# The first eight weight units of a hybrid mixer as two seven-product block multiplications, and convolution taps of two channel tiles by turns

## The chip, the core and the metric

The kernel runs on one core of a Trainium2 chip. The metric is the device time of one execution in microseconds (us), as the median of several runs. The engines of the core are named as in the profile: PE (TensorE, matmuls), PEld (its weight loads), DVE (VectorE), ACT (ScalarE), POOL (GpSimd) and SP (SyncE, which here only issues DMA transfers).

## The reference, cut to what matters

The program is a two-layer trunk for 512 frames and 16 meta tokens (T = 528) of width 1024, in float32. Each layer adds half a SwiGLU feed-forward, a mixer, and half a second feed-forward, each behind an RMSNorm.

```python
def hybrid_mixer(u, w_in, ...):
    proj = u @ w_in
    q, k, v, a, b, g_sb, g_conv = jnp.split(proj, IN_SPLITS, axis=-1)
    y_sb = stick_breaking_attention(q, k, v) @ w_attn_out
    y_conv = conformer_conv(a, b, conv_w, conv_b, conv_ln_g, conv_ln_b) @ w_conv_out
    m = jax.nn.sigmoid(g_sb) * y_sb + jax.nn.sigmoid(g_conv) * y_conv
    return m @ w_out
...
def conformer_conv(a, b, conv_w, conv_b, ln_g, ln_b):
    u = a * jax.nn.sigmoid(b)
    y = causal depthwise convolution of u, 31 taps, 512 channels, + conv_b
    return jax.nn.silu(layernorm(y, ln_g, ln_b))
```

The change concerns a and b, the value and gate halves of the GLU (512 channels each, four tiles of 128), and the 31 taps of the convolution behind it.

## The kernel before, in words

**Numbers in two halves.** Activations lie transposed: 128 channels by 528 tokens a tile, eight tiles u[0..7] for the width of 1024. Each operand of a matmul is split into a rounded part hi and a rest lo (`split`, L77: ScalarE copies hi, VectorE subtracts), and a product is three matmuls: hi·hi, hi·lo, lo·hi. Tokens go in two halves of 264 columns.

**Units.** Weights come as units, tiles of 128 x 8 x 128 (512 KB), listed in `units` (L130 to L155) in the order of use. `unit` (L243) hands out the next one and prepares up to three ahead (`LOOK`). `prep_unit` (L213) makes hi and lo in four buffers each (tags wh, wl). Mixer units get hi by a ScalarE copy (L224), a negated hi by another (L225), and an accumulating DMA from POOL's queue that adds the weight to it (L226), which is lo. Other units use `split`. `fetch` (L179) loads raw units through SP's queue into three buffers (tag wr), in the order of `fetches`.

**Seven products for eight.** From the third or fifth channel tile on, the feed-forwards multiply gate and up weights of two channel tiles as a 2 x 2 block system: two halves of the width by two channel tiles, against two halves of the width by two halves of the tokens. `quad` (L566) does this with seven products, w11, s1, s2, w21, s3, w22, s4 (`QUAD`), where the s are sums of weight blocks; each product is 2 x 4 x 3 = 24 matmuls (L580). `fetch_sums` (L196) loads s1 and s3 by a plain DMA (L208) and an accumulating one on POOL's queue (L210); s2 and s4 are further VectorE additions (L236). The sums of activations that they need are made by `sums` (L365): two ScalarE copies, four VectorE operations and two splits for each of four pairs of tiles. For the feed-forward behind a mixer, and for the one behind a whole layer, three of the four are made in the tail ahead of it (`prepare`, L326) and the last in `head` (L517), whose two plain tiles (L502) come ahead of the blocks.

**The mixer** (L678). At its start the residual h is stored to DRAM (L687). The GLU loop (L760 to L774) takes, for each of four channel tiles, unit b (both token halves, 48 matmuls, L706) and unit a (one half after the other, 48 matmuls, L720). After the first b the RMSNorm's scale is computed (L409, four matmuls with a matrix of ones, then `rsqrt`, L391). VectorE multiplies by that scale (L726), ScalarE takes the sigmoid, POOL multiplies (L773) into the padded tile uc. Then attention runs with the products q, k, v and the gates in its gaps, in an order of TensorE written out by hand (L987), and then the post stage (L998): last gate unit, attention output (ao, 4 units), the convolution's LayerNorm (L1029 to L1056), two gate units, convolution output, output projection.

**The taps.** `conv_some` (L736) issues VectorE's taps (L748, each multiplies a shifted uc by a column and adds y to it) at the lowest priority behind an evacuation: 31 taps of one channel tile after the other, about two for each evacuation of 264 columns (`CONV_STEP` = 4). What is left when the first attention-output unit is done (`AO_FIRST` = 1) comes before the LayerNorm (L1028). `constants` (L288) loads tables that attention needs; the first feed-forward calls it (L546).

Outside hand-written orders the compiler places the instructions of each engine in one queue, by priority and by its own estimate of when their inputs are ready.

Of the kernel before, what the change touches and what calls it, by code (L numbers as in the profile page):

```python
# [13 lines left out]
P = 128  # L14
# [19 lines left out]
CONV_STEP = 4  # L34
# [4 lines left out]
AO_FIRST = 1  # L39
# [21 lines left out]
def kernel(ctx, tc, hT, par, const, wg1, wu1, wd1, win, wao, wco, wout, wg2, wu2, wd2, out):  # L61
# [15 lines left out]
    def split(x, hi, lo):  # L77

        act.copy(hi, x)  # L79
        dve.tensor_tensor(out=lo, in0=x, in1=f(hi), op=ALU.subtract)  # L80

# [14 lines left out]
    def fn(out, in_, func, **kw):  # L96
# [8 lines left out]
        table["acts"].append(i)  # L105

# [3 lines left out]
    RAW_OF = {"w11": (0, 0), "w22": (1, 1), "w12": (0, 1), "w21": (1, 0)}  # L110
# [19 lines left out]
    units = []  # L130
    for l in range(DEPTH):
        for fi, (wg, wu, wd) in enumerate(((wg1, wu1, wd1), (wg2, wu2, wd2))):
            if fi == 1:
                for i in range(4):
                    units += [(("b", l, i), win[l, 16 + i], 8), (("a", l, i), win[l, 12 + i], 8)]
# [23 lines left out]
    ready, raws, spared = {}, {}, set()  # L159
    quads = {"pool": None, "of": None}  # L160

    def pieces(n, block=None):

        key, src, nk = units[n]
        if nk in QUAD:
            wg, wu, m = src
            k, c = RAW_OF[block or nk]
            return [(4 * e, 4 * e + 4, w[m + c, :, 4 * k:4 * k + 4]) for e, w in enumerate((wg, wu))]
# [3 lines left out]
    fetches = []  # L172
    for n, (key, src, nk) in enumerate(units):
        if nk == "w11":
            fetches += [n, n + 5, n + 3]
        elif nk not in QUAD:
            fetches.append(n)

    def fetch(spare=None):  # L179

        while state["fetch"] < len(fetches) and (spare or state["out"] < RAW):
            n = fetches[state["fetch"]]
            state["fetch"] += 1
            if spare:
                raw = spare
                spared.add(units[n][0])
            else:
                state["out"] += 1
                raw = wpool.tile([P, 8, P], F32, tag="wr", bufs=RAW, name="wr")
            for a, b, src in pieces(n):  # L190
                nc.sync.dma_start(raw[:, a:b], src)
            raws[units[n][0]] = raw
            if spare:
                return

    def fetch_sums():  # L196

        n = state["sums"]
        while n < len(units) and units[n][2] != "w11":
            n += 1  # L200
        if n == len(units) or units[n][0][1:3] != quads["of"]:
            return
        state["sums"] = n + 1
        _, *at = units[n][0]
        for name, first in (("s1", "w11"), ("s3", "w22")):
            t = quads["pool"].tile([P, 8, P], F32, tag=name, bufs=2, name=name)
            for a, b, src in pieces(n, first):
                nc.sync.dma_start(t[:, a:b], src)  # L208
            for a, b, src in pieces(n, "w12"):
                pool.dma_start(t[:, a:b], src, accum_op=ALU.add)  # L210
            raws[(name, *at)] = t

    def prep_unit():  # L213
# [7 lines left out]
        if nk not in QUAD:  # L221
            raw = raws.pop(key)
            if key[0] in MIXER:
# [925 lines left out]
```

## Time and profile before

| | us |
|---|---|
| runs of the kernel before | 2151.03, 2152.31, 2152.36 |
| their median | 2152.31 |
| span of the profiled execution | 2150.5 |
| mixer's GLU stage in layer 0, first to last matmul | 368.3 to 415.5 |
| the same in layer 1 | 1445.2 to 1492.4 |

The profiled execution's own time is its span, 2150.5 us, and the little before its first and behind its last instruction. The first table of the profile lists the busy time of each engine and the number of its instructions. A list of waits says which engine waited for whom. The chain of waits follows the work that ended last back through what released it. A table by stretches gives, for a stretch of the span, each engine's busy time (x instructions), the granted TensorE clock, the mean busy share of the 16 DMA engines and GB/s. A timeline row is start, length, engine, line, operation, out<-in, and in brackets the idle time before it with what ended that. For groups of DMA transfers the time to landing runs from issue to the last byte.

### The profile page before, as it was taken

The page shows a single profiled execution, that of the slowest core. Times are in us where ns is not written, and L with a number is a line of the kernel's source. Part 1 is how long each engine was busy: PE and PEld are TensorE (multiplying, and loading weights), DVE is VectorE, ACT ScalarE, POOL GpSimd, SP SyncE. Part 2 cuts the span into 40 slices and gives each one's busy share as a digit, 9 for nine tenths or more (in the row PEclk, how much of TensorE's full clock was granted, in tenths as well). Part 3 has the DMA queues.
Part 4 walks back from the last instruction along what each step waited for, and adds up shares of the span by engine and source line. Part 5 has one row for each costly group of instructions (what it writes and reads, how often), then busy time and mean ns, then how long its engine had stood idle before and what let it go on. Part 6 is the DMA issues. An engine that isn't in the chain of part 4 may idle for free.

```text
span 2150.5 us, 39932 instructions
## 1 busy us (share of the span) xinstructions
PE 2135.9 (99%) x16226; PEld 2052.8 (95%) x16226; DVE 1521.5 (71%) x2091; ACT 1137.9 (53%) x1587; POOL 488.7 (23%) x449
## 2 busy tenths in 40 slices
PE   9999999999999999999999999999999999999998
PEld 9999999999999999999999999999888889999897
DVE  7867685677766777677877676856677767767685
ACT  6434355467776545343554443554778775444354
POOL 1322321211111131313113223212112111322320
PEclk9999999999999999999999999999999999999999
DMA  8465536865578747464365655368656886665542
GB/s 236 133 165 141 142 104 198 181 138 119 134 169 180 175 129 189 129 161 122 99 169 145 168 140 146 103 193 184 142 127 133 187 188 167 159 175 143 144 111 77
DMA packets 140168, 324.90 MB, mean 151 GB/s; under 512 B 15568, under 2 KB 19664, under 8 KB 139984
## 3 DMA queue, kind: packets, MB, share of 16 engines
q1 hardware_dynamic: 101856, 226.36, 33.3%
q0 software_dynamic: 37440, 95.44, 26.1%
q8 instruction: 127, 2.08, 0.4%
q10 hardware_dynamic: 688, 0.55, 0.1%
q14 instruction: 57, 0.47, 0.1%
HBM read 315.86 MB, written 6.42 MB: 150 GB/s over the span
## 4 chain that ended last, share of the span: by engine, by line
PE 99%; ACT 0%; DVE 0%; DMA 0%; issue 0%; DVEq 0%; ACTq 0%
PE pb L580 16%; PE ps L580 16%; PE ps L720 15%; PE ps L260 12%; PE ps L706 10%; PE pe L260 6%; PE pb L260 6%; PE pe L580 5%; PE z L706 2%; PE ps L502 2%; PE pe L502 1%; PE pb L502 1%; PE z L877 1%; PE po L921 1%; PE z L900 1%; PE ps L554 1%
## 5 line engine op out<-in xcount | busy, mean ns | idle before, releaser
L79 ACT CAST wh<-wr 128x1024 fp32r<-128x1024 f32 (+4 forms) x275 | 242.2, 887 | 372.4 <-PE ps L260 94.5
L80 DVE TENSOR_TENSOR wl<-wr,wh 128x1024 fp32r<-128x1024 f32 (+4 forms) x275 | 300.6, 1096 | 57.4 <-ACT wh L79 53.5
L79 ACT CAST wh<-s 128x1024 fp32r<-128x1024 f32 x158 | 165.8, 1049 | 274.9 <-DVE s L236 83.1
L80 DVE TENSOR_TENSOR wl<-s,wh 128x1024 fp32r<-128x1024 f32 x158 | 216.1, 1368 | 59.4 <-ACT wh L79 58.7
L720 PE MATMUL ps<-uh,wh 128*128 128x264 f32 (+1 forms) x792 | 243.8, 308 | 0.0
L720 PE MATMUL ps<-uh,wl 128*128 128x264 f32 (+1 forms) x792 | 240.0, 303 | 0.0
L720 PE MATMUL ps<-ul,wh 128*128 128x264 f32 (+1 forms) x792 | 239.9, 303 | 0.0
L640 POOL TENSOR_TENSOR h<-h,dt 128x528 f32<-128x528 f32 (+1 forms) x96 | 179.9, 1879 | 258.1 <-DVE dt L638 255.2
L210 POOL DMA_DIRECT2D s<-wg x78 | 72.8, 938 | 596.9 <-DMA s<-wg 337.9
L748 DVE SCALAR_TENSOR_TENSOR y<-uc,prm,y 128x528 f32<-128x528 f32 (+1 forms) x240 | 197.7, 824 | 4.1
L224 ACT CAST wh<-wr 128x1024 fp32r<-128x1024 f32 x104 | 109.1, 1049 | 141.2 <-issue 46.9
L580 PE MATMUL ps<-ul,wh 128*128 128x264 f32 (+1 forms) x624 | 177.4, 284 | 0.0
L580 PE MATMUL pb<-sl,wh 128*128 128x264 f32 (+1 forms) x624 | 176.9, 283 | 0.0
L580 PE MATMUL ps<-uh,wl 128*128 128x264 f32 (+1 forms) x624 | 176.9, 283 | 0.0
L580 PE MATMUL pb<-sh,wl 128*128 128x264 f32 (+1 forms) x624 | 176.8, 283 | 0.0
L580 PE MATMUL pb<-sh,wh 128*128 128x264 f32 (+1 forms) x624 | 176.5, 283 | 0.0
L580 PE MATMUL ps<-uh,wh 128*128 128x264 f32 (+1 forms) x624 | 176.2, 282 | 0.0
L720 PEld LDWEIGHTS ps<-uh,wl 128*128 128x128 f32 x792 | 149.1, 188 | 5.9
L720 PEld LDWEIGHTS ps<-uh,wh 128*128 128x128 f32 x792 | 148.9, 188 | 5.4
L720 PEld LDWEIGHTS ps<-ul,wh 128*128 128x128 f32 x792 | 149.0, 188 | 5.1
L260 PE MATMUL ps<-ah,wh 128*128 128x264 f32 (+1 forms) x616 | 142.0, 300 | 0.0
L260 PE MATMUL ps<-ah,wl 128*128 128x264 f32 (+1 forms) x616 | 141.8, 300 | 0.0
(319 smaller groups left out, 6460.8 us busy)
## 6 DMA issues: line engine op xcount, KB each, us to landing
wr<-wd SPq DMA_DIRECT2D x96, 384.0 KB, 3.6
wr<-win SPq DMA_DIRECT2D x72, 512.0 KB, 4.4
wl<-win POOLq DMA_DIRECT2D x72, 512.0 KB, 7.8
wr<-wg SPq DMA_DIRECT2D x117, 256.0 KB, 3.0
wr<-wu SPq DMA_DIRECT2D x117, 256.0 KB, 3.4
s<-wg SPq DMA_DIRECT2D x78, 256.0 KB, 5.2
s<-wu SPq DMA_DIRECT2D x78, 256.0 KB, 5.7
s<-wg POOLq DMA_DIRECT2D x78, 256.0 KB, 5.2
```

Source lines behind the costliest of these rows:

```text
L79: act.copy(hi, x)
L80: dve.tensor_tensor(out=lo, in0=x, in1=f(hi), op=ALU.subtract)
L210: pool.dma_start(t[:, a:b], src, accum_op=ALU.add)
L224: act.copy(hi[:, :nk], raw[:, :nk])
L260: pe.matmul(ps[:, c, :n], wt[:, k0 + k, :], xt[:, s:s + n], start=(k == 0 and pi == 0), stop=(k == end and pi == 2))
L502: pe.matmul(ps[:, e, :TH], wt[:, k, :], xt[:, s], start=(k == ORDER[0] and pi == 0), stop=(k == ORDER[-1] and pi == 2))
L554: pe.matmul(ps[:, e, :TH], wt[:, k, :], xt[:, s], start=(k == 0 and pi == 0), stop=(k == KD - 1 and pi == 2))
L580: pe.matmul(ps[:, e, :TH], wt[:, 4 * e + kk, :], xt, start=start and kk == 0 and pi == 0, stop=kk == 3 and pi == 2, skip_group_check=True)
L640: pool.tensor_tensor(out=tri(h[j], mode), in0=tri(h[j], mode), in1=tri(t, mode), op=ALU.add)
L706: pe.matmul(ps, wt[:, k0 + k, :], xt[:, s], start=(n == 0 and pi == 0), stop=(n == nk - 1 and pi == 2))
L720: pe.matmul(ps, wt[:, k, :], xt[:, s], start=(n == 0 and pi == 0), stop=(n == KD - 1 and pi == 2))
L748: t = dve.scalar_tensor_tensor(out=y, in0=uc[i][:, c0 + k:k + T], scalar=col(w0 + k), in1=y, op0=ALU.mult, op1=ALU.add)
```

## The change

It does four things.

1. The eight GLU units of a layer become two block systems of the kind above: pair 0 has channel tiles 0 and 1, pair 1 has 2 and 3, with gate (b) in the place of gate and value (a) in that of up. The seven products of both pairs are interleaved in one hand-written order (`OPENING`), 14 products of 24 matmuls. The unit names o11 and o21 stand for w11 and w21 where they are loaded as plain units. The norm's matmuls come between the two first products and the third.
2. The sums that the blocks need are made in the tail of the feed-forward ahead (three pairs) and behind the norm (the last).
3. Taps go by turns between the two channel tiles of a pair, and start when a pair is done; `CONV_STEP` is 5 and `AO_FIRST` 2.
4. `constants` is called in the mixer of layer 0 into a temporary tile, not in the first feed-forward; identity is loaded apart.

```diff
-CONV_STEP = 4
+URGENT = 200
+CONV_STEP = 5
...
-AO_FIRST = 1
+AO_FIRST = 2
...
+    OPENING = (("o11", 0), ("o11", 1), ("o21", 0), ("s1", 0), ("s2", 0), ("o21", 1), ("w22", 0), ("s3", 0), ("s1", 1),
+               ("s4", 0), ("s2", 1), ("s3", 1), ("w22", 1), ("s4", 1))
...
-                for i in range(4):
-                    units += [(("b", l, i), win[l, 16 + i], 8), (("a", l, i), win[l, 12 + i], 8)]
+                units += open_pair((2, l), [(win[l, 16:20], win[l, 12:16], m) for m in (0, 2)])
...
     for n, (key, src, nk) in enumerate(units):
+        at = key[1:]
         if nk == "w11":
-            fetches += [n, n + 5, n + 3]
+            later_sums.append((n, ("s1", "s3")))
+            fetches += [(n, (name, *at), name) for name in ("w11", "w22", "w21")]
+        elif nk == "s1" and at in opened:
+            first = units[n - 1][2] in OPEN
+            later_sums.append((n, ("s3",) if first else ("s1", "s3")))
+            fetches += [(n, key, nk)] if first else []
+        elif at in opened and nk in ("s2", "s4"):
+            fetches.append((n, ("w22" if nk == "s2" else "w21", *at), "w22" if nk == "s2" else "w21"))
         elif nk not in QUAD:
-            fetches.append(n)
+            fetches.append((n, key, nk))
+
+    def load(raw, n, *blocks):
+
+        for queue, block, kw in zip((nc.sync, pool), blocks, ({}, {"accum_op": ALU.add})):
+            for a, b, src in pieces(n, block):
+                queue.dma_start(raw[:, a:b], src, **kw)
...
-            if key[0] in MIXER:
+            raw, nk0, nk = raws[key], nk, 8 if nk in OPEN else nk
+            if key[0] in MIXER or nk0 == "o11" or nk0 == "o21" and units[n - 1][2] == "o11":
                 act.copy(hi[:, :nk], raw[:, :nk])
                 act.activation(lo[:, :nk], raw[:, :nk], AF.Copy, scale=-1.0)
-                pool.dma_start(lo[:, :nk], src[:, :nk].bitcast(F32R), accum_op=ALU.add)
+                for a, b, src in pieces(n):
+                    pool.dma_start(lo[:, a:b], src.bitcast(F32R), accum_op=ALU.add)
...
-            split(raws[("s1" if nk in ("s2", "s4") else nk, *at)], hi, lo)
+            i = split(raws[("s1" if nk in ("s2", "s4") else nk, *at)], hi, lo)
+            if nk == "s3" and at in opened:
+                tc.add_manual_dep(i.ins, state["rsqrt"].ins.name, NOSYNC, reason="behind the norm")
...
+    def pair(ptile, sp, st, mode, of, ats, between, take, done):
...
+        As = [ptile() for _ in range(2)]
+        ws = [unit("o11", *of, at) for at in ats]
+        for ks in (range(KH - 1), (KH - 1,)):
+            for A, w in zip(As, ws):
+                products(A, w, x(0, 0), True, ks)
+        Bs = [ptile("pb")]
+        begin(Bs[0], v(As[0]))
+        between(ptile("pe"), copies[0])
+        Bs.append(kept(As[1]))
+        q, E, c22 = {}, {}, {}
+
+        def step(name, n):
+            w = unit(name, *of, ats[n])
+            if name == "o21":
+                products(As[n], w, x(0, 1))
+                take(n, As[n], 0, 0)
+            elif name == "s1":
+                G = ptile() if n else ptile("pe")
+                products(G, w, sx(0), True)
+                q[n] = kept(G)
+            elif name == "s2":
+                if n:
+                    keep, Bs[n] = Bs[n], ptile()
+                    begin(Bs[n], keep)
+                products(Bs[n], w, sx(1))
+                E[n] = ptile("pe")
+                opposite(E[n], Bs[n], q[n])
+            elif name == "s3":
+                products(Bs[n], w, sx(2))
+                c22[n] = sp.tile([P, 2, TH], F32, tag="c22", bufs=2, name="c22")
+                opposite(c22[n], Bs[n], q[n])
+                take(n, c22[n], 1, 1)
+            elif name == "w22":
+                products(E[n], w, sx(3))
+                take(n, E[n], 1, 0)
+            else:
+                done(n, 1)
+                products(Bs[n], w, x(1, 1))
+                take(n, Bs[n], 0, 1)
+                done(n, 0)
+
+        for name, n in OPENING[2:]:
+            step(name, n)
...
-            todo = [(i, k) for i in range(4) for k in range(TAPS)]
+            todo = [(i, k) for p in (0, 2) for k in range(TAPS) for i in (p, p + 1)]
...
+                def between(pn, behind):
+                    rs["r"] = npool.tile([P, T], F32, tag="rstd", bufs=1, name="rstd")
+                    with priority(-URGENT):
+                        rms_rstd(glu, st, pn, FULL, rs["r"])
+                    sums(lambda: glu.tile([P, T], F32, tag="g", bufs=3, name="g"), 3, st, FULL, behind)
...
+                    dve.tensor_tensor(out=x[:, a:b], in0=c[:, 0, :HALF], in1=rs["r"][:, a:b], op=ALU.mult)
+                    last_evac[0] = dve.tensor_tensor(out=y[:, PAD + a:PAD + b], in0=c[:, 1, :HALF], in1=rs["r"][:, a:b],
+                                                     op=ALU.mult)
+                    fn(x[:, a:b], x[:, a:b], AF.Sigmoid)
+                    pool.tensor_tensor(out=y[:, PAD + a:PAD + b], in0=y[:, PAD + a:PAD + b], in1=x[:, a:b], op=ALU.mult)
+                    conv_some(CONV_STEP, last_evac[0])
...
+                quads.update(pool=glu, of=(2, l))
+                if l == 0:
+                    constants(glu)
+                fetch_sums()
+                with tc.manual_schedule(engines={mybir.EngineType.PE}):
+                    pair(btile, glu, st, FULL, (2, l), (0, 2), between, take, done)
+                quads["pool"] = None
...
-        ffn(l, 0, st, FULL, lambda tp, j, _: prepare(tp, j, base + KD, st1))
+        ffn(l, 0, st, FULL, lambda tp, j, alloc: prepare(tp, j, base + KD, st1, FULL, alloc))
```

In the opening s1 of pair 0 is fetched as a raw unit with a plain and an accumulating load; s3 of pair 0 and s1 and s3 of pair 1 are loaded into the opening's own buffers. Each pair's last evacuation hands its two tiles to the taps.

159 lines of the change are left out of this document (100 added, 59 removed).

## The prediction

> **What bounds the kernel now.** I read the engine totals first, then who TensorE waited for, then the chain of waits, then the DMA share of the stage that changes.
>
> ```profile
> span 2150.5 us, 39932 instructions
> PE 2135.9 (99%) x16226; PEld 2052.8 (95%) x16226; DVE 1521.5 (71%) x2091; ACT 1137.9 (53%) x1587; POOL 488.7 (23%) x449
> ```
> ```profile
> PE ps L554 <- ACT wh L79: 4.8, 1, 4.8
> ```
>
> TensorE (PE) is busy for 99% of the span, and the longest list of its waits has one that counts, 4.8 us before its first matmul. So no wait is there to be removed: time goes down only with matmuls, and goes up with every wait the change creates. The mixer's opening, the stage that changes, in the chain of waits (start, length, what); the last row is the same point in layer 1:
>
> ```profile
> 368.33 5.83 PE z L706 x48
> 374.16 0.48 PE z L409 x4
> 374.65 5.85 PE ps L720 x48
> ```
> ```profile
> 1445.20 5.83 PE z L706 x48
> ```
>
> 48 matmuls of 264 columns take 5.84 us: 0.1217 us each, back to back (the 284 ns that groups list for one include the pipeline). Eight units of 48 and the four norm matmuls (L409) fill 368.3 to 415.5.
>
> The DMA queues over the whole execution (MB, share of 16 engines' time), then stretches of the span; busy us of PE, weight loads, VectorE, ScalarE and POOL with their counts, and last the clock, DMA share and GB/s:
>
> ```profile
> q1 hardware_dynamic: 101856, 226.36, 33.3%
> q0 software_dynamic: 37440, 95.44, 26.1%
> ```
> ```profile
> 333.00:368.33 35.33, 35.33 (x293) 35.33 (x292) 20.38 (x29) 21.46 (x30) 4.97 (x6) 1.00 0.69 207
> ...
> 355.00:368.33 13.33, 13.33 (x113) 13.33 (x112) 6.28 (x9) 9.71 (x13) 2.74 (x4) 1.00 0.90 255
> 368.33:380.00 11.67, 11.67 (x99) 11.67 (x98) 6.20 (x10) 8.11 (x10) 1.71 (x2) 1.00 0.99 252
> ...
> 1051.00:1087.56 36.56, 36.56 (x302) 36.56 (x301) 30.78 (x50) 23.59 (x37) 2.65 (x2) 1.00 0.37 114
> ```
>
> The opening is the stage where DMA is nearest its limit: 0.90 and 0.99 around its first matmul. A MB on q1 (plain loads) costs 716 us / 226.36 = 3.16 us of all engines, one on q0 (accumulating loads) 561 / 95.44 = 5.88 us. So a 512 KB tile costs 1.66 us plain, 3.08 accumulating, 4.74 for both.
>
> **The change part by part.** *Removed matmuls.* Eight units of 48 (384) become 14 products of 2 x 4 x 3 = 24 (336). 48 fewer x 0.1217 = 5.84 us a layer, all on the path; two layers **-11.7 us**. The norm's four matmuls stay.
>
> *Opening order.* Call the stage's first matmul 0. Products begin: o11 of both pairs 0 (in turns), norm 5.84, o21_0 6.33, s1_0 9.25, s2_0 12.17, o21_1 15.1, w22_0 18.0, s3_0 20.9, s1_1 23.9, then 2.92 each to 41.4. A plain unit lasted 5.84, so preparation has half the time per unit.
>
> *Norm at 5.84.* Before, VectorE finished its input at 372.88 + 0.71 = 373.6 for the matmuls at 374.16. The feed-forward head of before, whose tail already makes three of the sums that the change adds here, shows the same step:
>
> ```profile
> 372.88 0.71 DVE L80 TENSOR_TENSOR nt<-nsum,nt 128x528 fp32r<-128x528 f32 x1 [0.70 <-ACT nt L79]
> ```
> ```profile
> 1087.56 5.83 PE pb L502 x48
> ```
> ```profile
> 1092.20 0.71 DVE L80 TENSOR_TENSOR nt<-nsum,nt 128x528 fp32r<-128x528 f32 x1
> ...
> 1094.57 1.22 DVE L80 TENSOR_TENSOR wl<-wr,wh 128x1024 fp32r<-128x1024 f32 x1
> ...
> 1099.78 0.71 DVE L512 TENSOR_TENSOR g<-pb,rstd 128x528 f32<-128x528 f32 x1
> ...
> 1108.64 1.22 DVE L236 TENSOR_TENSOR s<-s,wr 128x1024 f32<-128x1024 f32 x1
> ```
>
> There it is done 5.35 us after the head's first matmul (1087.56): in time. So the sums moved into the tail, 12 multiply-subtracts and 6 splits, cost nothing: with them VectorE was busy 30.8 of 36.6 us (1051 to 1087.56), without them 20.4 of 35.3 (333 to 368), and TensorE never stopped. Without that cover they would cost their VectorE time, about 10 us a layer. The block tiles of PSUM and the copies (B, q) go to ScalarE, busy 8.1 of 11.7 us there: 0.
>
> *VectorE behind the norm.* In that head it worked without a pause to 1099.78 + 0.71 = 1100.5, 12.9 after the start. Here it has one add more (1.22) and one evacuation less (0.71) before s2_0 can use its low part: 13.4 against 12.4 needed. Wait 0 to 1.0; I take 0, since the second half of the last sum and the first evacuation can come after it.
>
> *o21_0.* Its low part comes by an accumulating load, which was issued in before at 366.07, or -2.3:
>
> ```profile
> 366.07 0.86 POOL L226 DMA_DIRECT2D wl<-win  x1 [3.48 <-ACT wl L225]
> ```
> ```profile
> 386.11 1.05 ACT L224 CAST wh<-wr 128x1024 fp32r<-128x1024 f32 x1 [3.32 <-PE z L706]
> ```
> ```profile
> 388.42 0.86 POOL L226 DMA_DIRECT2D wl<-win  x1 [4.20 <-ACT wl L225]
> ```
> ```profile
> L226 POOL DMA_DIRECT2D wl<-win x9: 856/857/881, 370.4 to 418.7; - x9
> DMA to landing us min/median/max: 7.0/8.0/8.9
> ```
>
> Landing after 7.0 to 8.9 is 4.7 to 6.6; its third matmul needs it at 6.6, just in time. But now the accumulating load of s1_0 goes ahead of it on POOL's queue (3.08 us of DMA). Wait 0 to 3.1, I take 1.0, as it shares that time with plain loads.
>
> *First q unit.* It is prepared when the product four before it ends, three products ahead: 3 x 2.92 + 0.24 = 9.0 us until its low part is used (before: 17.5). Cast to issue took 388.42 - 386.11 = 2.3; with the landing 9.3 to 11.2. Wait 0.3 to 2.2, taken 1.3 (the median landing). TensorE's order is fixed there and nothing runs in its place, so it is paid in full. By the rule of the Trainium skill (SBUF — State Buffer, Who interferes with whom) a VectorE instruction in a two-port mode keeps GpSimd from writing descriptors until it ends. By it an issue could wait for one whole VectorE instruction, 1.2 us, and the sum would be 2.4 us higher; the rows' issues of 0.86 us with little spread show no such hold, and I go by the rows.
>
> *Loads of s3_0, s1_1, s3_1.* They start when the tail's buffers are free, in the head of before at 1091.53, 3.97 after its first matmul, and the first was in use here:
>
> ```profile
> 1091.53 0.33 SPq L208 DMA_DIRECT2D s<-wg  x1
> ```
> ```profile
> 1105.80 1.05 ACT L79 CAST wh<-s 128x1024 fp32r<-128x1024 f32 x1 [7.66 <-DMA s<-wu]
> ```
> ```profile
> 1112.00:1116.00 4.00, 4.00 (x35) 4.00 (x34) 3.97 (x6) 2.55 (x4) 0.00 (x0) 1.00 0.02 3
> ```
>
> That cast is at 18.2, and by 1112 the DMA engines were idle. Here s3_0's cast must start by 18.6 (product less cast and low part, 2.3) and s1_1's by 21.6. Wait 0 to 7.4 (worked out below), taken 0: three tiles instead of four share the DMA engines.
>
> *Constants.* Two transfers that the opening has to move beside the weights, the stores of h and the constants:
>
> ```profile
> keep<-h SPq DMA_DIRECT2D x16, 264.0 KB, 4.2
> ...
> cc<-const SPq DMA_DIRECT2D x1, 392.0 KB, 7.7
> ```
>
> The constants move from the first feed-forward to layer 0's opening: on SyncE behind the last stores of h and ahead of s3_0, 0.40 MB or 1.3 us of DMA. The wait that it could cause lies within the ranges above; what it leaves waited for nothing.
>
> *Taps by turns.* Three taps on one y and three independent instructions of the same width:
>
> ```profile
> 387.63 2.38 DVE L748 SCALAR_TENSOR_TENSOR y<-uc,prm,y 128x528 f32<-128x528 f32 x3
> ...
> 652.89 2.13 DVE L1050 SCALAR_TENSOR_TENSOR y<-y,prm,lr 128x528 f32<-128x528 f32 x3
> ```
>
> 0.79 against 0.71 each: by turns 248 taps may save 20 us of VectorE, but nobody waits for taps: 0. They start later (15 of a layer's 124 in the opening, not 24), so in layer 0 nine are left for the post stage, 7 us of VectorE. Its chain before:
>
> ```profile
> 617.25 11.73 PE ps L706 x96
> 628.98 0.89 PE ps_ln L1032 x4
> 629.87 17.60 PE ps L706 x144
> 647.47 0.89 PE ps_ln L387 x4
> ```
>
> With two attention-output units first, 17.6 us lie ahead of the LayerNorm's first matmuls and 11.7 between them and the second. VectorE's last taps and its last sum of squares:
>
> ```profile
> 615.98 1.56 DVE L748 SCALAR_TENSOR_TENSOR y<-uc,prm,y 128x528 f32<-128x528 f32 x2
> ...
> 634.29 0.70 DVE L1016 TENSOR_TENSOR lsum<-lsum,lsq 128x528 f32<-128x528 f32 x1
> ```
>
> The taps ended at 617.5, and 7 us more stay ahead of 617.3 + 17.6; the sums of squares end 5.1 us behind the first matmuls and fit into 11.7. Cost 0; without that cover 7 us.
>
> *Sum.* TensorE has no wait to lose in these stages, so none of the bounds lies below nothing. Per layer -5.84 + 1.0 + 1.3 = -3.5; two layers -7.1 on a span of 2150.5, to 2143.4. The median of the runs, 2152.31, is 1.8 above the span (start and end lie around it): **2145.2 us**.
>
> **The rivals.** *Nothing waits* (0.12): -11.7, 2140.6. For it: orders and depths could fit. Against: the q unit's 9.0 us against 9.3 at best.
>
> *DMA becomes the bound* (0.14). A pair of pairs needs seven tiles with both loads and five plain: 7 x 4.74 + 5 x 1.66 = 41.5 us of DMA in 41.4 of TensorE; before it was 37.9 in 46.7. From -6.5 to s1_1's cast at 21.6 (28.1 us) have to be moved: five accumulating loads (s1_0, o11_1, o21_0, s3_0, s1_1) 15.4, seven plain 11.6, three stores of h at 0.86, 2.6, and the constants 1.3: 30.9. Late by 2.8 a layer, beside the waits taken: 2145.2 + 5.6 = 2150.8, no difference. Against: the share counts overlap, and exceeds 1.0 in places.
>
> *Slower: all s tiles land together and the clock falls* (0.11). In the head all accumulating loads were in flight at once and were through at about 1112, 24.4 after the start. There that cost nothing. Here three tiles (14.2) with o21_0's accumulating load, three plain and the constants make some 23.6 us of DMA against four tiles' 19.0: landed 4.6 later, at 29.0, s1_1 is 7.4 late. After its one idle stretch TensorE is slow:
>
> ```profile
> 4.83 0.81 PE L554 MATMUL ps<-uh,wh 128*128 128x264 f32 x2 [4.83 <-ACT wh L79]
> ...
> 10.45 0.64 PE L554 MATMUL ps<-uh,wl 128*128 128x264 f32 x2
> 10.89 0.47 PE L554 MATMUL ps<-ul,wh 128*128 128x264 f32 x2
> ```
>
> two matmuls in 0.44 us instead of 0.24; the 26 from 4.83 to 10.89 lost 6.06 - 26 x 0.1217 = 2.9 us. 7.4 + 2.9 - 5.84 = +4.5 a layer: 2161.3. It decides where s1_1's accumulation lands over 27.4 us after the first matmul (without the slow clock). The Trainium skill (TensorE: Matmul & The Clock Gate, What's actually happening) states that an idle window of about 3.4 us halves the clock; this trace has only the start to show it, and agrees there.
>
> *The change does not cut matmuls* (0.03): 2152.3; the list of 14 products speaks against it.
>
> **How the numbers follow.** The forecast's case has 0.60: 2142.6 to 2148, waits between 1 and 3.7 a layer. A measurement of this kernel can tell about 0.2%, 4.3 us, from no change. Faster: 0.60 + 0.12 = 0.72. Same: 0.14 + 0.03 = 0.17. Slower: 0.11. Range 2140.0 to 2155.0: from nothing waits (less a little spread) into the slower case's beginning; about 0.1 is left above it.
>
> **What would show it.** Matmuls 16226 - 96 = 16130. TensorE's waits: about 1 us before o21_0 and 1.3 before the first q unit, in both layers, put down to DMA. DMA share near 1.0 through the opening. Taps at about 0.71 us each in pairs. LayerNorm without a wait. I am wrong if waits in an opening pass 5.84 us, if VectorE or ScalarE is what ends them, or if a wait stands in attention or the post stage.

## The result: slower, 2165.2 us where 2145.2 was forecast

| | us |
|---|---|
| changed kernel, five runs | 2164.46 to 2169.95, median 2165.17 |
| kernel before, on the same chip, five runs | 2151.03 to 2152.36, median 2152.28 |
| ratio | 1.0069, 95% interval 1.0057 to 1.0081 |
| profiled execution of the changed kernel | 2169.65, span 2167.9 |

Runs of the changed kernel lie up to 5 us apart, and the profiled one is at the upper end; TensorE runs at half its clock behind some of its waits, and for how long differs from run to run (66 slow matmuls in this profile, 88 in that of a_again, at spans of 2167.9 and 2167.6).

The profile after, first its span, the engines' busy time and the group of the taps; the last row is the same group before:

```profile
span 2167.9 us, 39999 instructions
...
PE 2133.3 (98%) x16130; PEld 2048.4 (94%) x16130; DVE 1572.5 (73%) x2185; ACT 1162.0 (54%) x1639; POOL 511.0 (24%) x469
...
L870 DVE SCALAR_TENSOR_TENSOR y<-uc,prm,y 128x528 f32<-128x528 f32 (+1 forms) x240 | 185.9, 810 | 0.5
```
```profile
L748 DVE SCALAR_TENSOR_TENSOR y<-uc,prm,y 128x528 f32<-128x528 f32 (+1 forms) x240 | 197.7, 824 | 4.1
```

The 96 matmuls are gone (16226 to 16130), and the span is 17.4 us longer. TensorE's list of waits (who waits, for whom: us in total, times, longest), where before only one entry counted. It counts idle time; where the text gives a wait 0.1 to 0.2 us longer, it is counted from the start of one matmul to the start of the next, less 0.12:

```profile
PE be L441 <- DVE be L459: 9.0, 2, 5.1
PE bs L441 <- DMA wl<-win: 5.4, 4, 2.6
PE ps L676 <- ACT wh L80: 4.9, 1, 4.9
PE bs L441 <- DVE be L459: 2.0, 2, 1.0
PE ps L290 <- ACT ah L80: 1.6, 1, 1.6
PE be L441 <- DVE nt L517: 0.7, 1, 0.7
PE ps L842 <- DVE q L942: 0.7, 1, 0.7
PE bs L441 <- ACT bb L452: 0.6, 2, 0.3
PE ps L290 <- DVE al L81: 0.4, 1, 0.4
```

The line L676 is the old one at the start. L441 is a product of the opening, L290 one of the first feed-forward, L842 a q or k unit. A name like s4_0 means product s4 of pair 0; B0 and B1 are the sums that the two pairs build up in PSUM, and q in VectorE's rows is the kept copy of product s1. The largest entry is VectorE's, not a DMA's: `be L459` is what is called the opposite here, q less B, which VectorE writes into the PSUM tile onto which w22_0 then adds. VectorE at that moment in layer 0 (start, length, and in brackets its idle time and what ended it):

```profile
393.11 0.43 DVE L459 SCALAR_TENSOR_TENSOR be<-bb,q 128x264 f32<-128x264 f32 x1
398.45 1.23 DVE L265 TENSOR_TENSOR wr<-wr 128x1024 f32<-128x1024 f32 x1 [4.91 <-DMA wr<-win]
399.59 0.43 DVE L459 SCALAR_TENSOR_TENSOR be<-bb,q 128x264 f32<-128x264 f32 x1
```

The opposite has two halves of 0.43 us. Between them in VectorE's queue stands an addition for a later unit (L265, the sum s4_0), which waits 4.91 us for its weights. The second half, whose inputs were ready, stands behind it, and TensorE with it. In layer 1 the addition waits 4.58 us at the same place. The Trainium skill (Perfetto Trace Analysis, Tensor Engine Instruction (MATMUL, LD_WEIGHTS)) says that the queues of VectorE, ScalarE and GpSimd are strictly first in, first out; these three rows agree.

The same stretches as rows of busy time (PE, PEld, DVE, ACT, POOL, then granted clock, DMA share, GB/s):

```profile
372.00:376.00 4.00, 2.96 (x25) 2.75 (x23) 1.94 (x5) 1.33 (x3) 0.39 (x5) 1.00 1.10 249
...
396.00:400.00 4.00, 0.00 (x0) 0.00 (x0) 1.55 (x3) 0.88 (x2) 0.00 (x0) 1.00 0.68 212
400.00:404.00 4.00, 3.83 (x19) 3.86 (x20) 4.00 (x6) 1.26 (x2) 1.45 (x1) 0.57 0.37 137
```

From 396 to 400 TensorE does nothing; in the next 4 us it gets through 19 matmuls, where 4 us by 0.1217 hold 33, at a granted clock of 0.57. DMA is at its limit around 372, but at 0.37 by 400.

The first wait of an opening is that of the second o11 (2.1 us; 2.8 in layer 1, and 0.8 and 0.5 more for the second half of the unit) for its low part, an accumulating load. POOL's queue:

```profile
361.56 1.78 POOL L255 DMA_DIRECT2D wl<-win  x2 [19.30 <-ACT wl L253]
366.30 1.75 POOL L205 DMA_DIRECT2D wr<-win  x2 [2.96 <-DMA wr<-win]
367.53 2.29 POOL L255 DMA_DIRECT2D wl<-win  x2
```

The second row is s1_0's accumulating load, which waited until its plain load had landed; the third is the low part of the second o11 behind it. ScalarE's copy for that one was ready at 365.8, so the queue held it for 1.7 us; its two halves then took 9.2 and 10.7 us to land. In the first feed-forward it is VectorE's queue again:

```profile
44.41 0.23 DVE L330 CAST identb<-ident 128x128 bf16<-128x128 f32 x1 [8.53 <-DMA ident<-const]
```

The copy of the identity waits 8.53 us for the identity's load, which took 11.7 us from issue to landing, and the work of the feed-forward stands behind it.

**The balance**, from the gaps between the starts of successive matmuls: waits and slow matmuls together cost 4.1 us in the first feed-forward, 13.4 in layer 0's opening with the first q and k units, 13.2 in layer 1's. With -11.7 for the missing matmuls this gives +19.0 for a measured +17.4.

### The profile page after: what moved, and what is told of

It is laid out like the page before. It is cut to its first block, busy times and chain, and to the rows that moved or that the text cites. A ratio compares the mean times of both kernels' runs of the same rounds, so it can differ in the third digit from the quotient of the medians.

```text
span 2167.9 us, 39999 instructions
## 1 busy us (share of the span) xinstructions
PE 2133.3 (98%) x16130; PEld 2048.4 (94%) x16130; DVE 1572.5 (73%) x2185; ACT 1162.0 (54%) x1639; POOL 511.0 (24%) x469
## 4 chain that ended last, share of the span: by engine, by line
PE 93%; DMA 3%; DVE 2%; ACT 1%; issue 0%; SPq 0%; DVEq 0%; ACTq 0%
PE pb L702 16%; PE ps L702 16%; PE ps L842 13%; PE ps L290 12%; PE ps L828 10%; PE pb L290 6%; PE pe L290 5%; PE pe L702 5%; PE ps L624 2%; DMA wr<-win 1%; PE z L1024 1%; PE bs L441 1%; PE po L1068 1%; PE z L1047 1%; PE pe L624 1%; PE pb L624 1%
## 5 line engine op out<-in xcount | busy, mean ns | idle before, releaser
L80 ACT CAST wh<-wr 128x1024 fp32r<-128x1024 f32 (+4 forms) x287 | 254.8, 894 | 379.3 <-PE ps L290 95.0
L81 DVE TENSOR_TENSOR wl<-wr,wh 128x1024 fp32r<-128x1024 f32 (+4 forms) x287 | 313.6, 1095 | 64.2 <-ACT wh L80 60.6
L81 DVE TENSOR_TENSOR wl<-s,wh 128x1024 fp32r<-128x1024 f32 x168 | 228.3, 1359 | 59.5 <-ACT wh L80 58.5
L842 PE MATMUL ps<-uh,wh 128*128 128x264 f32 (+1 forms) x664 | 207.9, 313 | 0.7 <-DVE q L942 0.7
L842 PE MATMUL ps<-ul,wh 128*128 128x264 f32 (+1 forms) x664 | 203.7, 307 | 0.0
L842 PE MATMUL ps<-uh,wl 128*128 128x264 f32 (+1 forms) x664 | 203.5, 306 | 0.0
L870 DVE SCALAR_TENSOR_TENSOR y<-uc,prm,y 128x528 f32<-128x528 f32 (+1 forms) x240 | 185.9, 810 | 0.5
L702 PE MATMUL ps<-ul,wh 128*128 128x264 f32 (+1 forms) x624 | 177.4, 284 | 0.0
L702 PE MATMUL ps<-uh,wl 128*128 128x264 f32 (+1 forms) x624 | 176.9, 283 | 0.0
L702 PE MATMUL ps<-uh,wh 128*128 128x264 f32 (+1 forms) x624 | 176.1, 282 | 0.0
L290 PE MATMUL ps<-ah,wh 128*128 128x264 f32 (+1 forms) x616 | 142.6, 301 | 1.6 <-ACT ah L80 1.6
L290 PE MATMUL ps<-al,wh 128*128 128x264 f32 (+1 forms) x616 | 142.3, 301 | 0.4 <-DVE al L81 0.4
L290 PE MATMUL ps<-ah,wl 128*128 128x264 f32 (+1 forms) x616 | 142.4, 301 | 0.0
L842 PEld LDWEIGHTS ps<-uh,wh 128*128 128x128 f32 x664 | 124.9, 188 | 6.5 <-issue 0.9
L842 PEld LDWEIGHTS ps<-uh,wl 128*128 128x128 f32 x664 | 125.0, 188 | 5.9
```

What stands on the lines that cost most here:

```text
L80: i = act.copy(hi, x)
L290: pe.matmul(ps[:, c, :n], wt[:, k0 + k, :], xt[:, s:s + n], start=(k == 0 and pi == 0), stop=(k == end and pi == 2))
L702: pe.matmul(ps[:, e, :TH], wt[:, 4 * e + kk, :], xt, start=start and kk == 0 and pi == 0, stop=kk == 3 and pi == 2, skip_group_check=True)
L842: pe.matmul(ps, wt[:, k, :], xt[:, s], start=(n == 0 and pi == 0), stop=(n == KD - 1 and pi == 2))
L870: t = dve.scalar_tensor_tensor(out=y, in0=uc[i][:, c0 + k:k + T], scalar=col(w0 + k), in1=y, op0=ALU.mult, op1=ALU.add)
```

## The experiments

**Theory (queues).** Each engine works its queue in order. In several places an instruction that waits for a late load stands ahead of one that TensorE needs: an addition and the identity copy on VectorE, an accumulating load on POOL, and perhaps casts on ScalarE. The loads themselves come early enough for the products that use them. **Rival (DMA).** The opening needs more DMA than its time holds (prediction's 41.5 in 41.4 us), so that waits removed in one place come back in another.

### One queue at a time

*e1_adds*: an order alone, the additions queued behind both halves of the opposite.

```diff
-                dve.tensor_tensor(out=x, in0=x, in1=y, op=ALU.add)
+                s = dve.tensor_tensor(out=x, in0=x, in1=y, op=ALU.add)
+                if at in opened and "opposite" in state:
+                    tc.add_manual_dep(s.ins, state["opposite"].ins.name, NOSYNC, reason="behind the opposite")
...
```

> The changed kernel with one thing different: VectorE's additions that make the second and fourth sums of a pair are queued behind both halves of the latest opposite (B's negative plus q). Theory of the queues: the 5.2 and 4.1 us that TensorE waits before w22_0 are no lateness of a load that TensorE needs, but an addition whose load is late and that stands ahead of the second half of the opposite on VectorE. Both waits and the slow clock behind them (1.7 and 2.4 us) go: about 13 us less than the changed kernel, near 2152 us. Rival, DMA as the bound: the load of w21_0 is simply late, so the wait moves to s1_1 or s4_0, 8.8 us further on, and the time stays within 3 us of 2165.

Measured 2157.1 us (ratio to before 1.0024, interval 1.0015 to 1.0033), 8.0 below the changed kernel. The waits of 5.1 and 3.9 us are gone:

```profile
PE bs L443 <- DMA wl<-win: 5.4, 4, 2.2
PE ps L678 <- ACT wh L80: 4.8, 1, 4.8
PE bb L443 <- DVE c L461: 2.1, 2, 1.3
PE bs L443 <- DVE be L461: 2.0, 2, 1.0
...
```

The load of the addition lands no earlier, 25.7 us after the opening's first matmul against 26.0 in the changed kernel; VectorE still waits for it, 1.38 us in layer 0, but both halves of the opposite are done by then. A smaller wait comes in place, `c L461` (2.1 in all), the next opposite, which stands at the end of 6.4 us of VectorE's work without a pause. The gain is 8.0 us, not the expected 13.

*e2_acc*: s1_0's accumulating load queued on POOL behind that of the second o11.

```diff
-            load(raw, n, *(("w11", "w12") if block == "s1" else (block,)))
+            load(raw, n, "w11" if block == "s1" else block)
+            if block == "s1":
+                state["owed"] = (raw, n)
...
-                    pool.dma_start(lo[:, a:b], src.bitcast(F32R), accum_op=ALU.add)
+                    i = pool.dma_start(lo[:, a:b], src.bitcast(F32R), accum_op=ALU.add)
+                if nk0 == "o11" and units[n - 1][2] == "o11":
+                    raw1, n1 = state.pop("owed")
+                    for a, b, src in pieces(n1, "w12"):
+                        d = pool.dma_start(raw1[:, a:b], src, accum_op=ALU.add)
+                        tc.add_manual_dep(d.ins, i.ins.name, NOSYNC, reason="behind the plain unit")
```

> The changed kernel with one thing different: the accumulating load of s1_0 is queued on POOL behind that of o11_1, not ahead of it. Theory of the queues: o11_1's load is issued near -6 instead of -0.6 and the wait of 2.1 us (layer 0) and 2.8 us (layer 1) in the second o11 product goes, with the slow clock behind it in layer 1 (1.5): 5 to 6 us less than the changed kernel, if the later waits stay. Rival, DMA as the bound: the 3.08 us of s1_0 are only moved, s1_0's product waits in its place and the time stays within 1 us. A third way: TensorE comes earlier to w22_0, whose wait then grows by what was saved, and the time stays for that reason.

Measured 2166.2 us (1.0070, 1.0054 to 1.0085): no gain. The wait of the second o11 is gone (its load is issued 6.3 us ahead of the opening's first matmul, in the changed kernel 4.8, not the 0.6 of the expectation), and the norm waits instead, 10.2 us in the two layers together, for ScalarE. ScalarE's queue:

```profile
374.73 1.04 ACT L80 CAST wh<-wr 128x1024 fp32r<-128x1024 f32 x1 [6.72 <-DMA wr<-win]
375.68 0.73 ACT L359 ACTIVATE uh<-h,prm 128x528 fp32r<-128x528 f32 x1
376.32 0.63 ACT L374 ACTIVATE sq<-h 128x528 f32<-128x528 f32 x1
378.36 0.63 ACT L80 CAST nt<-nsum 128x528 fp32r<-128x528 f32 x1 [1.42 <-DVE nsum L382]
```

The cast of s1_0 waits 6.72 us for that load and stands ahead of the norm's cast. The wait went from POOL's queue into ScalarE's. The waits for the opposite fell from 9.0 to 2.8 us, as TensorE came there later. By this run alone the rival would do as well: something is late wherever one looks.

*e5_noacc*: the changed kernel with that load left out, so that s1 of pair 0 lacks one of its two weight terms in both layers.

```diff
-            load(raw, n, *(("w11", "w12") if block == "s1" else (block,)))
+            load(raw, n, "w11" if block == "s1" else block)
```

> The changed kernel with the accumulating load of s1_0 left out in both layers (the block sum of pair 0 lacks one of its two terms). Theory: this one load, waiting on GpSimd's queue and followed by ScalarE's wait for it, is what held the low part of the second o11 (2.1 and 2.8 us) in the changed kernel and the norm (5.0 and 5.5 us) where it was put behind; without it both are absent, and the waits for the opposite (5.2 and 4.1) stay as they are: 2159 to 2162 us. Rival, the DMA engines are simply behind in the head: 1.6 MB less to move does not show at the second o11, whose low part stays 1 to 3 us late; 2164 us.

Measured 2158.9 us (1.0034, 1.0021 to 1.0047). Both waits are absent (behind the norm 0.6 us a layer stays), with 1.05 MB less on POOL's queue in the whole execution, not the expectation's 1.6; the opposite's stay at 4.5 and 4.0, and s1_0 waits 1.7 us for VectorE in layer 0. One load had caused the one wait or the other, by where it stood.

*e4_ident*: the identity copy queued behind the tail of the first feed-forward.

```diff
-            dve.tensor_copy(identb, ident)
+            i = dve.tensor_copy(identb, ident)
+            tc.add_manual_dep(i.ins, state["ul"].ins.name, NOSYNC, reason="behind the feed-forward")
...
```

> The changed kernel with one thing different: the copy of the identity to bfloat16 is queued on VectorE behind the tail of the first feed-forward. Theory: in the changed kernel this copy stands early in the first feed-forward and holds VectorE until the identity's load lands, 11.7 us after its issue, so that TensorE waits 2.4 us near 58 us; that wait goes and nothing else changes: 2.4 us less. Rival: the wait near 58 us comes from the load itself delaying the weights, and it stays.

Measured 2164.3 us (1.0060, 1.0046 to 1.0074); the two waits of the first feed-forward are gone from the profile. The medians differ by 0.9 us only, less than the runs of the changed kernel spread, so that what these waits cost in time is not shown.

*e3_end*: s2_1 ahead of s4_0 in the hand-written order.

```diff
-               ("s4", 0), ("s2", 1), ("s3", 1), ("w22", 1), ("s4", 1))
+               ("s2", 1), ("s4", 0), ("s3", 1), ("w22", 1), ("s4", 1))
```

> The changed kernel with s2 of pair 1 ahead of s4 of pair 0 in the opening's order, so that one product stands between an opposite, which reads B1, and s3 of pair 1, which adds to B1. Theory: the waits of 1.17 us a layer go, 2.3 us below the changed kernel's time; all other waits stay. Rival: the opposite ends late for another reason (VectorE behind with its queue), and the wait stays or moves to s4 of pair 0; no difference.

Measured 2157.5 us (1.0026, 1.0017 to 1.0035), 7.6 below the changed kernel in place of 2.3. The waits of 1.17 us did shrink (0.44 and 0.53), but most of the gain has another reason, seen in VectorE's queue:

```profile
390.08 0.90 DVE L459 SCALAR_TENSOR_TENSOR be<-bb,q 128x264 f32<-128x264 f32 x2
392.62 1.22 DVE L81 TENSOR_TENSOR wl<-s,wh 128x1024 fp32r<-128x1024 f32 x1 [1.64 <-ACT wh L80]
395.63 1.23 DVE L265 TENSOR_TENSOR s<-s,wr 128x1024 f32<-128x1024 f32 x1 [1.78 <-DMA wr<-win]
```

With two products exchanged the compiler placed both halves of the opposite together, ahead of the addition. The theory of the expectation was right about its own 1.17 us and blind to this: here the change of TensorE's order reordered VectorE's queue as well.

*e6_taps*: the taps in sequence.

```diff
-            todo = [(i, k) for p in (0, 2) for k in range(TAPS) for i in (p, p + 1)]
+            todo = [(i, k) for i in range(4) for k in range(TAPS)]
```

> The changed kernel with the convolution's taps one channel tile after the other in place of two by turns. Theory: nobody waits for taps, VectorE is busy about 12 us longer and the time stays within 1 us of the changed kernel's. Rival: by turns the taps take VectorE out of the way of the opposite and the sums, and in sequence the time is 2 us or more longer.

Measured 2169.9 us (1.0087, 1.0073 to 1.0101), 4.7 above the changed kernel's median, though its four runs (2169.5 to 2171.6) touch the other's range. VectorE is 10.5 us busier (1583.0). The waits of q units for an evacuation grew from 0.7 to 2.9 us in all; what makes the rest isn't settled. "Nobody waits for taps" is wrong by some 2 us at least.

*a_again*: the changed kernel once more, beside e3_end and two later kernels.

> The changed kernel once more, on the same chip as the others. Its runs stood at two levels, near 2164.7 and 2169.8 us. If the 5 us are stretches of TensorE at half speed behind waits that are the same in all runs, both levels come again, and a profile from the lower one has the same waits and fewer slow matmuls; if they are another length of waits, its waits differ by as much.

Measured 2165.9 us (1.0069, 1.0056 to 1.0081); the five runs spread from 2164.3 to 2169.4 without two clear levels, and the profiled one was again at the upper end, so what sets the spread is left open.

### The queues one after the other

*f_all*: e1, e2, e3 and e4 together.

> The changed kernel with the three edits of the other runs of this call, and the second sum's product of pair 1 taken ahead of the fourth of pair 0, so that a product lies between the opposite that reads B of pair 1 and the product that writes it (1.2 us of wait a layer). Theory of the queues: of about 21 us of waits in the two openings some 3 to 6 are left, and the 2.4 us near 58 us are gone: 2165 - 13 - 5.5 - 2.4 - 2.3 = about 2142 us, faster than the kernel before by 8 to 10 us. Rival, DMA as the bound: the openings still wait 8 us or more in all, put down to loads, and the time is 2150 us or more.

Measured 2158.9 us (1.0037, 1.0024 to 1.0050), far above the expected 2142. What is left is the norm (10.4 us in the two layers, as in e2) and the first q unit, 2.0 and 1.3 us for its low part: the wait that the prediction had put at 0.3 to 2.2.

*f2_norm* turns the norm's cast and s1_0's cast round on ScalarE.

```diff
+            if nk == "s1" and at in opened and units[n - 1][2] in OPEN:
+                tc.add_manual_dep(i.ins, state["nt"].ins.name, NOSYNC, reason="behind the norm's copy")
...
+                with priority(-URGENT):
+                    parts = norm_parts(glu, st, FULL)
...
```

> Starts from f_all; the split of the norm's input is written out before the opening's first units, and ScalarE's cast of s1_0 is queued behind the norm's cast. Queue theory: in f_all the norm waited 5.2 and 5.6 us only because its cast stood behind s1_0's cast, which waited 6.85 us for its accumulating load; with the order turned round these waits go, and with them the slow matmuls behind them: 10.8 less in waits and 2 to 4 less in slow matmuls, 2143 to 2147 us, faster than the kernel before. s1_0 itself may then wait 0 to 3 us for its load. DMA rival: the loads themselves are too late, and at least 8 us of waits come back at s1_0, s3_0 or s1_1; 2152 us or more.

Measured 2156.5 us (1.0024, 1.0015 to 1.0033), far above the expected 2143 to 2147. The norm's waits are gone. The product behind it waits instead, 2.4 and 3.3 us, and the first q unit now 4.3 and 1.6. By the number this is the rival's. By the releaser half of it is: the q unit waits for a DMA, the product behind the norm for ScalarE.

*f3_q* makes the first q unit's low part by VectorE, without an accumulating load.

```diff
-            if key[0] in MIXER or nk0 == "o11" or nk0 == "o21" and units[n - 1][2] == "o11":
+            if key[0] in MIXER and (key[0], key[2]) != ("q", 0) or nk0 == "o11" or nk0 == "o21" and units[n - 1][2] == "o11":
```

> f2_norm, and the low part of the first q unit of each layer is made by VectorE (loaded value less its rounded copy) in place of an accumulating load. If the q unit's wait in f_all (2.0 and 1.3 us) is the path cast, issue, landing, as the prediction had it, it goes: 3.3 us below f2_norm, 2140 to 2144. If the plain load of that unit is what is late, the wait stays at 2.0 and 1.3 and the time is that of f2_norm.

Measured 2151.3 us (0.9997, 0.9988 to 1.0006), not the expected 2140 to 2144. The wait of the q unit for its low part went in both layers. What waits behind the norm (o21_0, for the copy of the o11 product into B0), and ScalarE's queue there:

```profile
PE bs L453 <- ACT bb L464: 5.6, 2, 3.1
```
```profile
371.65 0.64 ACT L80 CAST nt<-nsum 128x528 fp32r<-128x528 f32 x1 [0.97 <-DVE nsum L387]
374.37 1.05 ACT L80 CAST wh<-wr 128x1024 fp32r<-128x1024 f32 x1 [2.08 <-DMA wr<-win]
...
376.14 0.59 ACT L464 COPY bb<-bs 128x528 f32<-128x528 f32 x1
```

It is s1_0's load for the third time: its cast, moved behind the norm's, now stands and waits ahead of the copy.

*f4_copies* queues it behind the two copies too, and layer 0's copies of constants behind the first opposite. *f5_taps3* also puts three taps in place of five behind each evacuation of the opening.

```diff
+        tc.add_manual_dep(state["s1"].ins, copies[1].ins.name, NOSYNC, reason="behind the copies")
...
-                    conv_some(CONV_STEP, last_evac[0])
+                    conv_some(3, last_evac[0])
```

> f3_q, with ScalarE's cast of s1_0 queued behind its two copies of the o11 products (it stood ahead of them and waited 2.08 us for its load), and layer 0's copies of the constants queued behind the first opposite. Queue theory: the waits of 2.6 and 3.3 us right behind the norm and the 2.4 us of slow matmuls behind the second go; s1_0 may wait up to 1 us instead. 2143 to 2146 us, faster than the kernel before. DMA rival: what is gained there comes back at s1_0 or s3_0, because their loads are what is late: 2149 us or more.

> f4_copies with three taps in place of five queued behind each evacuation of the opening. In f3_q the first q evacuation stood behind five taps (3.87 us) and TensorE waited 1.6 us for it in layer 0. Two taps less are 1.5 us: that wait nearly goes, 1 to 1.6 us below f4_copies; the six taps per layer that are left over cost nothing in the post stage. Rival: the q evacuation waits for the products of its own unit and taps do not matter; no difference.

Measured 2151.0 us (0.9998, 0.9989 to 1.0007) and 2148.2 us (0.9984, 0.9975 to 0.9993). f4 missed its range: the product behind the norm no longer waits for its copy, but o21_0's low part is late. f5 gained 2.8, more than the expected 1 to 1.6. In f5:

```profile
...
PE bs L455 <- DMA wl<-win: 4.2, 3, 2.5
PE bs L455 <- ACT bs L466: 2.8, 2, 1.7
PE bb L455 <- DVE wl L81: 0.3, 1, 0.3
```

The first row is the accumulating load of o21_0. On POOL's queue it waited only 0.67 us, for ScalarE's copy; its halves then took 10.1 and 11.7 us to land. This wait is the load's own.

*f6_b1* writes the copy of B1 (second row above) out earlier, with its PSUM tile; *f7_o21* also makes o21_0's low part by VectorE; *f9_o21* is f5 with that step alone.

```diff
                 take(n, As[n], 0, 0)
+                if n:
+                    keep, Bs[n] = Bs[n], ptile()
+                    begin(Bs[n], keep)
...
             elif name == "s2":
-                if n:
-                    keep, Bs[n] = Bs[n], ptile()
-                    begin(Bs[n], keep)
...
-            if key[0] in MIXER and (key[0], key[2]) != ("q", 0) or nk0 == "o11" or nk0 == "o21" and units[n - 1][2] == "o11":
+            if key[0] in MIXER and (key[0], key[2]) != ("q", 0) or nk0 == "o11":
```

> f5_taps3, with the copy of B1 into its PSUM tile written out right behind the evacuation of o21 of pair 1, so that it stands ahead of the casts of s4_0 and s2_1 in ScalarE's queue (in f5_taps3 it came at 398.24 and TensorE waited 1.85 us for it, 1.28 in layer 1). Queue theory: both waits go, 3.1 us below f5_taps3, 2145 us. DMA rival: s2_1 needs the sum whose term lands at 394.6, and the wait stays, put down to VectorE or DMA; no difference.

> f6_b1, with the low part of o21_0 made by VectorE in place of an accumulating load, in both layers. If the accumulating load is late because the DMA engines are at their limit there (share 1.1), its waits (1.5, 0.5 and 2.7 us with about 0.3 behind each) go and 3 us of DMA a layer with them: 4 to 5 us below f6_b1, 2140 to 2142. If the plain load of o21_0 is what is late, or VectorE's 1.2 us more push the norm or the sums back, 0 to 2 us are gained.

> f5_taps3 with the low part of o21_0 made by VectorE in place of an accumulating load in both layers, nothing else. From f7_o21: the waits for o21_0's low part (1.5, 0.5 and 2.7 us) and the slow matmuls behind them (some 2 us) go; VectorE is then what s1_0 and s2_0 wait for (2.2 us a layer, 4.4), and the waits for the copy of B1 (1.85 and 1.28) stay or shrink: 2143 to 2147 us, below f5_taps3's 2148.2. If the load's share of the DMA engines was not what held o21_0, nothing goes: 2148 us or more.

Measured: f6 2157.7 (1.0026, 1.0017 to 1.0035), f7 2148.8 (0.9986, 0.9977 to 0.9995), f9 2143.4 (0.9962, 0.9948 to 0.9976). f6 removed the wait for the copy of B1 and made a new one:

```profile
PE ps L862 <- ACT tmp L105: 6.1, 2, 3.3
```

The first q unit waits for work on the last GLU tile. That the earlier allocation turned round which PSUM buffers the following tiles get is the likely reason, but no run shows the buffers. f7 and f9 differ in this edit alone and lie 5.4 us apart, and f9 has no such wait. f9's page and its list of waits:

```profile
span 2140.8 us, 39985 instructions
...
PE 2122.8 (99%) x16130; PEld 2040.0 (95%) x16130; DVE 1577.4 (74%) x2189; ACT 1156.6 (54%) x1635; POOL 501.6 (23%) x463
```
```profile
PE ps L696 <- ACT wh L80: 4.9, 1, 4.9
PE bb L455 <- DVE wl L81: 2.8, 2, 1.4
PE be L455 <- DVE wl L81: 1.0, 2, 0.5
```

What is left is VectorE behind the norm, 0.7 us at s1_0 and 1.55 at s2_0 in each layer. No wait is a DMA's, though the DMA engines are as full in these 16 us of both layers as in the same part of the changed kernel's openings (1.03 and 0.97 there):

```profile
372.00:388.00 16.00, 14.11 (x113) 13.57 (x112) 14.71 (x22) 11.79 (x16) 6.43 (x7) 1.00 1.04 270
1444.00:1460.00 16.00, 14.10 (x113) 13.62 (x112) 15.07 (x22) 12.26 (x17) 6.38 (x7) 1.00 0.99 242
```

So full DMA engines alone don't make TensorE wait, and e1 and f2 show that orders alone, with every load kept, take 8.0 and 8.7 us off. The rival doesn't fall altogether. f9 is 21.8 us faster than the changed kernel: 11.8 of this came from steps that change orders and the number of taps alone (f_all and f2 8.7, f4 and f5 3.1), and 10.0 from the two that take away an accumulating load in each layer (f3 5.2, f9 4.8; at 3.08 us each by the prediction's price, 6.2 of its 41.5 us of DMA). Whether those two loads were late by the path from cast to landing or by the full DMA engines, no run separates; o21_0's landed late by about 2 us in layer 0 and 2.7 in layer 1 (f5). The version f9 beats both kernels, and the kernel before by 8.3 us.

## Why the prediction was wrong, step by step

- **Removed matmuls, -5.84 us a layer.** Right: 16130, and f9, with the waits nearly gone, has a span 9.7 below the kernel before.
- **Norm at 5.84, cost 0.** In the changed kernel nearly so (under 0.5 us), in part by luck: the second o11 had waited 2.9 us just ahead of it. The term rested on the row of another stage, in which no cast of a late tile was queued ahead of the norm's; e2 shows 5.0 and 5.5 us when one is.
- **VectorE behind the norm, 0 to 1.0, taken 0.** Mis-sized: 0.86 us at s1_0 in layer 0 of the changed kernel, and 2.2 a layer in f9 where nothing else hides it.
- **o21_0's low part, 0 to 3.1, taken 1.0.** Here the prediction saw that "the accumulating load of s1_0 goes ahead of it on POOL's queue", and priced this as DMA time. It missed that the instruction *waits* there for its own plain load (2.96 us of idle queue in the changed kernel), and that the second o11 is behind it, which waited 6.2 us in the two layers. o21_0's own wait, in f5, was 2.0 and 2.7: inside the range.
- **First q unit, 0.3 to 2.2, taken 1.3.** Right in f_all: 2.0 and 1.3, and gone in both layers when the accumulating load went (f3). The changed kernel hardly shows it, probably because its earlier waits gave the load time.
- **Loads of s3_0, s1_1, s3_1, 0 to 7.4, taken 0.** This is the step that failed. It compared landings with the start of the casts that use them, and priced VectorE's additions at their busy time (1.22 us). It did not ask what else stands behind a waiting instruction. The late load was in no term: the plain one for s4_0's sum, whose product comes three products behind w22_0. It held VectorE's queue, and with it w22_0: 5.1 and 3.9 us, and 4.2 us of slow matmuls behind. The load was late for two reasons that the prediction did not see either. SyncE issued it 16.6 us after the opening's first matmul, when VectorE had freed a buffer for it (7.4 us of waiting in SyncE's queue). Then its halves took 7.2 and 9.0 us to land with the DMA share at 1.01 (388 to 396 us); the next plain load, issued at 399.70 while the share fell, took 3.4 and 3.6.
- **Constants, "what it leaves waited for nothing".** Wrong: the move brought a copy on VectorE with it that waits for its load, 4.1 us in the first feed-forward of the profile with the slow matmuls (e4 gained 0.9 by the medians).
- **s3_1 right behind the opposite.** Not in the prediction at all: the opposite reads B1 and s3_1 adds to it, and no product stands between. 1.17 us in each layer.
- **Taps by turns.** VectorE's taps took 185.9 us in place of 197.7, 12 saved and not 20 (0.775 each, where the prediction looked for about 0.71). That nobody waits for taps was wrong at the first q units (0.9 us; f5 gained 2.8 with fewer taps there).
- **Rivals.** "Slower" had the right size (2161.3) by luck, with the wrong mechanism: not all s tiles late at s1_1, but single loads at the head of queues. Its slow clock was right. The list of what would show the forecast wrong held: waits over 5.84 us in an opening (9.6 us of idle time in layer 0's), and VectorE ending most of them (6.8).

Waits did not add up one by one: e1, e2, e4 and e5 each took the waits away that they aimed at, and what the time gained went from nothing (e2) to 8.0 (e1), as the next queue's wait came out from behind.

## What to carry to other kernels

When a change puts a late-loaded operand into an engine's queue, don't only ask whether the load lands before TensorE needs that operand; list what is queued behind the instruction that waits for it, on VectorE, ScalarE and POOL each, and price the wait at the first of those that TensorE needs. Moving such an instruction back by one place moves the wait to the next instruction that matters; queue it behind all of them. Where a compiler sets the order, a reordering of TensorE's work can reorder the other queues too (e3), so compare the queues and not only the sums.

## What the runs showed that was not expected

TensorE fell to half its clock after shorter pauses than the start of the kernel had suggested. In the changed kernel, waits of 1.6 and 0.45 us in the first feed-forward were followed by 15 matmuls at 0.22 us in place of 0.122 (granted clock 0.50 from 62.4 to 65.8 us); in f3_q a gap of 3.3 us was followed by some 27 such matmuls, one of 2.6 us by none, and in f5_taps3 one of 2.7 us by 14. The Trainium skill (TensorE: Matmul & The Clock Gate, What's actually happening) gives an idle window of about 3.4 us that runs free of the kernel; the case of 3.3 us nearly fits it, those of 2.7 us in f5_taps3 and the short ones in the first feed-forward do not by their length alone, and the measurement decides. Two gaps of nearly one length (2.6 and 2.7 us) came out differently, so length alone does not settle it. The slow matmuls are about 7 of the changed kernel's 30.7 us.

The DMA engines stood at a mean share of about 1.0 for 16 us in f9 and ended no wait of TensorE's. A full share does not say that anybody waits for the transfers.
